# One decoder step on one core: first phi matrix loaded whole with its bias ahead of the loop, norm scaled in place, modulation in pairs of blocks, four activation sums moved into the compression

## The chip, the cores and the metric

The kernel runs on one core of a Trainium2 chip. The metric is device microseconds from the start to the end of one execution. The time of the kernel before is the median of three runs, 1209.62 us (1209.15 to 1214.17). One further execution was profiled, and all rows of views below are from it. Lines (L658) are lines of the kernel before, unless the text says of the kernel after. The engines: TensorE (PE; its weight loads PEld), VectorE (DVE), ScalarE (ACT), GpSimd (POOL) and SyncE (SP), which issues most DMAs.

## What is computed

One inference step of a decoder layer, in f32: 512 prompt tokens and 8 x 4 sample tokens, 1024 features, 16 heads over 4 KV heads. Only the first part of it bears on the change:

```python
sh1, sc1, g1, sh2, sc2, g2 = split(silu(c) @ w_ada + b_ada)
h  = rmsnorm(x, norm1) * (1 + sc1) + sh1
bg, cg, xin, q, kc, vc, ks, vs, kw, vw, nsa_g, merge_g = split_columns(h @ w_in)

def compress(rows, pe, w1, w2):          # k and v of 8 cached sequences of 1024 rows
    halves = rows in strides of 16       # block i = halves i and i + 1
    blocks = concat(halves[:-1], halves[1:]) + pe
    return gelu(flat(blocks) @ w1) @ w2
```

What follows (a gated short convolution, three attention branches, the output projections and a SwiGLU FFN) is the same in both kernels.

## The kernel before, in words

All activations lie feature-major: xT is [128, 8, 544], feature block k by token, and the 544 columns are worked in two halves, 288 and 256 wide (HS). Most f32 products are made of three products of a high and a low part: to_hilo copies the high part on ScalarE (L394) and subtracts it on VectorE (L395). Large products go by pairs of blocks in a scheme of seven half-block products (seven, L284), which needs four sums of quarters of the activation, S0 to S3 (T_ in the code), each 128x1088 with a high and a low part.

**The start.** SyncE issues the DMAs in an order written by hand (queue, L223). phi_load (L577) brings wphi[v], the first compression matrix for k (v = 0) or v (v = 1), 1.05 MB each; hp is a small slab with the position encodings, the second compression matrices and the conditioning input; cmp_gather (L617) brings the eight cached pages of a sequence (0.26 MB each) by the page table, those of sequence 0 half by SyncE and half by ScalarE's queue. wake(n) (L689) multiplies the identity by a 128x512 view of it n times, work with no result that runs before the first data are there.

**The compression** is a loop over 16 steps n = (sequence b, v). A step is 24 products of 128x128 on TensorE (cmp_M, L652): 16 of the pages by the two halves of wphi[v], and 8 of xs (the sum of odd and even strides, cmp_sum, L646, VectorE) by wsum[v] (the sum of the two halves of wphi[v], phi_sum, L582, VectorE). Then cmp_finish (L660) adds the bias on ScalarE, forms the blocks on VectorE and takes the gelu on ScalarE, and cmp_out2 (L677) multiplies by the second matrix. The bias is pe @ w1: phi_bias (L585) makes it with 16 products pb and a copy pbs on VectorE (L591), and phi_bias2 (L593) with one more product pbt and a copy into pbias (L597). Between the steps TensorE also makes the adaLN products (mod_slab), slab after slab as they arrive.

**Norm and modulation** run beside the steps 6 to 15: square_acc on blocks of xT, the inverse root (inv_from_sums, L440), its broadcast over partitions (inv_bcast, L474), and then modulate (L488), block by block and half by half: VectorE multiplies by the inverse root and A (md_u, L493), ScalarE adds the shift (Identity with a bias, L498), to_hilo writes h_h and h_l.

**Behind the compression** comes the linear product of the attention gates (L869, 48 products with gate's high and low weights, a sigmoid on ScalarE), and then the first kv pair by the seven-product scheme, whose weights (wslab, prepare) are brought and split into wh, wl, Wh, Wl. sum_1 stands in step 14, sum_2 in step 15 and sum_3 and sum_4 behind the loop. ScalarE loads a table whenever it changes between gelu and sigmoid.

What sets the order on an engine: a scheduler places the instructions of each engine in one row, by when it expects their inputs; the engine then takes the row in order. An instruction that waits holds up all that stand behind it on its engine.

Of the kernel before, what the change touches and what calls it, by code (L numbers as in the profile page):

```python
# [20 lines left out]
KC = 8  # L21
TP = 512
TS = 32
# [133 lines left out]
def build(tc, a, o):  # L157
# [419 lines left out]
    def phi_load(v, taps=slice(0, 2)):  # L577

        ks = slice(8 * taps.start, 8 * taps.stop)
        queue(lambda: sync.dma_start(wphi[v][:, ks], a["wt"][SLAB_AT[("phi", v)]].rearrange("p (k f) -> p k f", k=16)[:, ks]))  # L580
# [19 lines left out]
    gat = mkpool(gst, "gat", side="right")  # L600
    wsum = [gat.tile([128, 8, 128], F32, name=f"wsum{j}") for j in range(2)]
# [106 lines left out]
    T_, st = [], []  # L708

    def sum_1():  # L710
        st.append(raw_tile("raw")[:, 0:4 * WH].rearrange("p (k n) -> p k n", k=4))
        dve.tensor_sub(st[0], fq(0, 0), fq(0, 1))
        to_hilo(st[0], *T_[0])

    def sum_2():
        dve.scalar_tensor_tensor(st[0], st[0], -1.0, fq(1, 1), ALU.mult, ALU.subtract)
        to_hilo(st[0], *T_[1])

    def sum_3():
        st[0] = raw_tile("raw")[:, 0:4 * WH].rearrange("p (k n) -> p k n", k=4)  # L720
        dve.tensor_sub(st[0], fq(1, 1), fq(0, 1))
        to_hilo(st[0], *T_[2])

    def sum_4():
        dve.tensor_add(st[0], st[0], fq(0, 0))
        dve.tensor_sub(st[0], st[0], fq(1, 0))
        to_hilo(st[0], *T_[3])

    STEPS = [(b, v) for b in range(8) for v in range(2)]
    for n, (b, v) in enumerate(STEPS):  # L730
# [1299 lines left out]
```

## Time and profile before

| | |
|---|---|
| runs, median of three | 1209.62 us |
| runs, lowest and highest | 1209.15, 1214.17 us |
| profiled execution | 1209.88 us |
| its span in the trace | 1208.1 us |
| mean granted clock of TensorE | 0.998 |
| matmul records | 10114 |

The span runs from the first to the last thing in the trace. An f32 product shows as two matmul records. In a row of the timeline the first number is the start, the second the time from there to the end of the last of the records that it groups (xN), and the bracket at the end names how long the engine had been idle and what released it. In a row of groups the number behind the bar is the busy time in us, then the mean of one in ns, then the idle time ahead. In a row of windows each engine has its busy time and number of instructions, then come the granted clock, the DMA engines' share and GB/s.

### The profile page before, as it was taken

The numbers are of one execution on the slowest core, as the hardware profiler recorded it, in microseconds if no ns is written. First come the engines' busy times: TensorE is split into PE (matmuls) and PEld (weight loads), VectorE is DVE, ScalarE is ACT, GpSimd is POOL, SyncE is SP. The second block draws the span as 40 slices with busy tenths as digits, with TensorE's granted clock in tenths as the row PEclk, the third lists the DMA queues.
The fourth block names the chain that finished last, engine by engine and source line by source line (L and its number), as shares of the span: only waits on it lengthen the run. The fifth ranks groups of instructions, "written<-read, shape, count | busy, mean of one in ns | idle before, by whom it ended". The sixth has DMA issues, their size and how long they took to land. (4 is left out here: it accounts for less than half of the span.)

```text
span 1208.1 us, 25725 instructions
## 1 busy us (share of the span) xinstructions
PE 1191.2 (99%) x10114; PEld 1096.6 (91%) x10114; DVE 849.8 (70%) x1927; ACT 647.6 (54%) x1302; POOL 101.7 (8%) x154
## 2 busy tenths in 40 slices
PE   9999999999999999999999999999999999999997
PEld 7999999999999888787777879999999999999996
DVE  2539976888775576686767866758746877876776
ACT  1416544565456333386766765528555666666542
POOL 1000240000000111120101100000020001001000
PEclk9999999999999999999999999999999999999999
DMA  9953655889655998979887878534475359439512
GB/s 325 370 223 124 203 167 161 261 237 251 201 176 191 365 327 299 312 203 264 234 222 216 220 209 285 201 126 167 110 182 197 136 181 262 149 129 252 197 53 75
DMA packets 82251, 255.63 MB, mean 212 GB/s; under 512 B 9032, under 2 KB 17096, under 8 KB 67930
## 3 DMA queue, kind: packets, MB, share of 16 engines
q1 hardware_dynamic: 69442, 229.85, 54.5%
q0 software_dynamic: 12112, 23.09, 11.7%
q8 instruction: 79, 1.29, 0.4%
q10 hardware_dynamic: 576, 1.05, 0.3%
q14 instruction: 42, 0.34, 0.1%
HBM read 223.15 MB, written 65.28 MB: 239 GB/s over the span
## 5 line engine op out<-in xcount | busy, mean ns | idle before, releaser
L301 ACT ACTIVATE work<-wA 128x272 f32<-128x272 f32 x153 | 60.0, 392 | 85.3 <-PE wA L254 81.5
L395 DVE TENSOR_TENSOR Wl<-ws,Wh 128x1024 fp32r<-128x1024 f32 (+1 forms) x51 | 60.7, 1190 | 47.3 <-ACT Wh L394 44.0
L1417 ACT ACTIVATE P<-P,nms 128x384 f32<-128x384 f32 (+3 forms) x120 | 65.0, 543 | 19.8 <-DVE nms L1416 19.1
L1416 DVE CUSTOM_DVE_ANT_0 P<-sp,ta 128x384 f32<-128x384 f32 (+3 forms) x120 | 52.1, 468 | 30.0 <-PE sp L1404 22.8
L252 PE MATMUL lin<-h_h,wh 128*128 128x288 f32 (+1 forms) x240 | 71.5, 298 | 0.0
L395 DVE TENSOR_TENSOR wl<-ws,wh 128x1024 fp32r<-128x1024 f32 (+1 forms) x51 | 60.3, 1182 | 15.8 <-ACT wh L394 14.6
L253 PE MATMUL lin<-h_l,wh 128*128 128x288 f32 (+1 forms) x240 | 69.2, 289 | 0.0
L254 PE MATMUL lin<-h_h,wl 128*128 128x288 f32 (+1 forms) x240 | 68.9, 288 | 0.0
L394 ACT ACTIVATE wh<-raw 128x1024 fp32r<-128x1024 f32 (+2 forms) x55 | 55.4, 1007 | 24.1 <-PE wC L253 16.9
L394 ACT ACTIVATE Wh<-ws 128x1024 fp32r<-128x1024 f32 (+1 forms) x51 | 52.3, 1025 | 29.9 <-PE wC L253 29.2
L394 ACT ACTIVATE wh<-ws 128x1024 fp32r<-128x1024 f32 (+1 forms) x51 | 52.4, 1027 | 29.1 <-PE wB L253 27.4
L247 ACT ACTIVATE wh<-raw 128x1024 fp32r<-128x1024 f32 (+1 forms) x43 | 41.9, 973 | 43.3 <-PE lin L253 24.4
L395 DVE TENSOR_TENSOR wl<-raw,wh 128x1024 fp32r<-128x1024 f32 (+2 forms) x55 | 63.4, 1153 | 1.8 <-ACT wh L394 1.7
L658 PE MATMUL phi<-gt,wphi 128*128 128x128 f32 x512 | 61.4, 277 | 0.5 <-DMA gt<-in_cache_cmp 0.5
L658 PEld LDWEIGHTS phi<-gt,wphi 128*128 128x128 f32 x512 | 59.1, 192 | 2.7 <-DMA gt<-in_cache_cmp 1.3
L248 DVE TENSOR_TENSOR wl<-raw,wh 128x1024 fp32r<-128x1024 f32 (+1 forms) x43 | 48.2, 1121 | 16.9 <-ACT wh L247 16.4
L252 PE MATMUL wA<-S_hi,Wh 128*128 128x272 f32 x184 | 55.3, 301 | 1.7 <-ACT work L301 1.6
L557 POOL DMA_DIRECT2D pre<-in_wt x28 | 27.3, 977 | 331.0 <-DMA pre<-in_wt 331.0
L254 PE MATMUL wA<-S_hi,Wl 128*128 128x272 f32 x184 | 53.2, 289 | 0.0
L253 PE MATMUL wA<-S_lo,Wh 128*128 128x272 f32 x184 | 53.0, 288 | 0.0
L252 PEld LDWEIGHTS lin<-h_h,wh 128*128 128x128 f32 x240 | 45.6, 190 | 7.5 <-issue 6.2
L253 PEld LDWEIGHTS lin<-h_l,wh 128*128 128x128 f32 x240 | 45.2, 188 | 0.1
(583 smaller groups left out, 4365.6 us busy)
## 6 DMA issues: line engine op xcount, KB each, us to landing
raw<-in_wt SPq DMA_DIRECT2D x88, 1024.0 KB, 6.6
sraw<-in_cache_sel SPq DMA_DIRECT2D x64, 256.0 KB, 4.8
gt<-in_cache_cmp SPq DMA_DIRECT2D x60, 256.0 KB, 5.8
pre<-in_wt SPq DMA_DIRECT2D x20, 512.0 KB, 7.3
pre<-in_wt POOLq DMA_DIRECT2D x20, 512.0 KB, 7.1
ws<-pre SPq DMA_DIRECT2D x20, 512.0 KB, 3.4
raw<-in_wt SPq DMA_DIRECT2D x12, 768.0 KB, 5.7
wraw<-in_cache_winT SPq DMA_DIRECT2D x8, 1024.0 KB, 7.2
```

What stands on the lines that cost most here:

```text
L247: act.activation(oh, view, AF.Copy)
L248: dve.tensor_sub(ol, view, oh.bitcast(F32))
L252: pe.matmul(p, lhsT=wh[:, k, :], rhs=xh, start=start, stop=False, **kw)
L253: pe.matmul(p, lhsT=wh[:, k, :], rhs=xl, start=False, stop=False, **kw)
L254: pe.matmul(p, lhsT=wl[:, k, :], rhs=xh, start=False, stop=stop, **kw)
L301: o_.snap_ops.append(act.activation(t, p, AF.Copy))
L394: act.activation(hi, src, AF.Copy)
L395: return dve.tensor_sub(lo, src, hi.bitcast(F32))
L557: pool.dma_start(dst, src, accum_op=ALU.add)
L658: pe.matmul(po[:, c0:c0 + 128], lhsT=w[:, ch], rhs=x[:, :, ch * 16:ch * 16 + 16], start=(n_ == 0 and ch == 0), stop=(n_ == 2 and ch == 7))
L1416: p_ops.append(dve.tensor_tensor_reduce(out=t[:, 0:n], in0=sps[br], in1=t_dist[:, 512 - n:512], scale=-hs, scalar=3e38, op0=ALU.add, op1=A ...
L1417: e_ops.append(act.activation(t[:, 0:n], t[:, 0:n], AF.Exp, scale=-1.0, bias=nms[:, c:c + 1], accum_out=sums[:, c:c + 1]))
```

## The change

What it does, in the order of the program:

- phi_load brings wphi[0] whole and first; hp follows it, and then come the pages of sequence 0. Before, the first half of wphi[0] came ahead of the pages, and the second half and hp behind them.
- The bias of v = 0 is made ahead of the loop: five wakes, phi_sum(0), pb(0), two wakes, pbt(0), two wakes. Before, six and four wakes stood there, and both biases were made in steps 0 to 2.
- cmp_finish runs one step earlier (the list late is gone). Two of the gathered sequences (3 and 6) get a buffer in a pool of their own, gat2, which is closed at step 13.
- The squares are summed in steps 6 and 7, and the inverse root is taken at step 8. At step 9, xT is multiplied in place by the broadcast inverse root, two blocks at a time, for all tokens.
- modulate_x takes the place of modulate: ScalarE applies A and the shift in one Identity with a scale and a bias, and to_hilo runs once for two blocks.
- All four sums are made in the loop: S0 and S1 with their splits at step 13, S2 and S3 at step 14, the split of S3 at step 15. Each sum has a raw buffer ("st") of the three.

```diff
-    def phi_load(v, taps=slice(0, 2)):
-        ks = slice(8 * taps.start, 8 * taps.stop)
-        queue(lambda: sync.dma_start(wphi[v][:, ks], a["wt"][SLAB_AT[("phi", v)]].rearrange("p (k f) -> p k f", k=16)[:, ks]))
+    def phi_load(v):
+        queue(lambda: sync.dma_start(wphi[v].rearrange("p k f -> p (k f)"), a["wt"][SLAB_AT[("phi", v)]]))
...
-            t = gat.tile([128, 8, 512], F32, tag="gt", bufs=2, name=nm("gt"))
+            t = (gat2 if b in (3, 6) else gat).tile([128, 8, 512], F32, tag="gt", bufs=1, name=nm("gt"))
...
-    phi_load(0, slice(0, 1))
+    phi_load(0)
+    queue(lambda: sync.dma_start(hp, a["hp"]))
     cmp_gather(0)
-    phi_load(0, slice(1, 2))
-    queue(lambda: sync.dma_start(hp, a["hp"]))
     phi_load(1)
...
-    wake(6)
+    wake(5)
     phi_sum(0)
+    pb_ = phi_bias(0)
+    wake(2)
+    pb_()
     accs1 = [xp.tile([128, HW[hf]], F32, name=f"xacc{hf}") for hf in range(2)]
-    fins, late = [], []
+    fins = []
     xs_ = cmp_sum(0, 0)
-    wake(4)
+    wake(2)
...
+    def sums(i):
+        pool_ = mkpool(t7st, f"t7{i}")
+        T_.extend(sums_of(pool_, i + j) for j in range(2))
+        for j in range(2):
+            st[i + j] = raw_tile("st")[:, 0:4 * WH].rearrange("p (k n) -> p k n", k=4)
+        if i == 0:
+            dve.tensor_sub(raw_sum(0), fq(0, 0), fq(0, 1))
+            dve.scalar_tensor_tensor(raw_sum(1), raw_sum(0), -1.0, fq(1, 1), ALU.mult, ALU.subtract)
+        else:
+            dve.tensor_sub(raw_sum(2), fq(1, 1), fq(0, 1))
+            dve.tensor_add(raw_sum(3), raw_sum(2), fq(0, 0))
+            dve.tensor_sub(raw_sum(3), raw_sum(3), fq(1, 0))
+
+    def modulate_x(k, hf):
...
+        for kk in (k, k + 1):
+            act.activation(xT[:, kk, c], xT[:, kk, c], AF.Identity, scale=A1[:, kk, 0:1], bias=sh1[:, kk, 0:1])
+        ks = slice(k, k + 2)
+        to_hilo(xT[:, ks, c], hh_[:, ks, c], hl_[:, ks, c])
...
-        late.append((b, v, po))
-        if n < 2:
-            pb_ = phi_bias(n)
-            if n:
-                pb0()
-            pb0 = pb_
-        if n == 2:
-            pb0()
-        if n:
-            ready_ = late[:1] if n == 1 else late
-            late = late[len(ready_):]
-            fins = [cmp_finish(*z) for z in ready_]
+        if n == 0:
+            pb_ = phi_bias(1)
+        if n == 1:
+            pb_()
+        fins = [cmp_finish(b, v, po)]
...
+        if n == 8:
+            invs = [inv_from_sums(tok_sums(accs1[hf], hf), hf, xp) for hf in range(2)]
         if n == 9:
-            invs = [inv_from_sums(tok_sums(accs1[hf], hf), hf, xp) for hf in range(2)]
+            for hf in range(2):
+                inv = inv_bcast(invs[hf], hf, xp)
+                for k in range(0, KC, 2):
+                    xv = xT[:, k:k + 2, hcols(hf)]
+                    dve.tensor_mul(xv, xv, inv.rearrange("p (x n) -> p x n", x=1).broadcast_to([128, 2, HW[hf]]))
...
+        if n == 13:
+            gbst.close()
+            sums(0)
+            for i in range(2):
+                sum_split(i)
         if n == 14:
-            t7a = mkpool(t7st, "t7a")
-            T_ += [sums_of(t7a, 1), sums_of(t7a, 2)]
-            sum_1()
             wg = split(slab("gate"))
+            sums(2)
+            sum_split(2)
         if n == 15:
-            sum_2()
-            xst.close()
+            sum_split(3)
...
-    sum_3()
-    sum_4()
     linear(wg, h, lambda hf, p: act.activation(gT[0:48, hcols(hf)], p[0:48, :], AF.Sigmoid))
```

The change reorders three engines. The numbers behind the names below tell tiles of one name apart. On TensorE, at the start of the program, before (gt_1 is the pages of sequence 0, wphi0 the first phi matrix):

```order
L694 MATMUL wake_8_289<-ident_66 128x512 x6
L694 MATMUL wake_10_301<-ident_66 128x512 x4
L658 MATMUL phi_11_307<-gt_1_171,wphi0_156 128x128 x16
L658 MATMUL phi_11_307<-xs_9_299,wsum0_164 128x128 x8
L589 MATMUL pb_13_335<-wphi0_156,hp_158 32x128 x16
L658 MATMUL phi_15_354<-gt_1_171,wphi1_157 128x128 x16
```

And on TensorE at the same place in the kernel after:

```order
L693 MATMUL wake_8_291<-ident_66 128x512 x5
L587 MATMUL pb_9_298<-wphi0_156,hp_158 32x128 x16
L693 MATMUL wake_11_317<-ident_66 128x512 x2
L594 MATMUL pbt_12_320<-sel_159,pbs_10_315 128x1
L693 MATMUL wake_14_327<-ident_66 128x512 x2
L657 MATMUL phi_15_331<-gt_1_175,wphi0_156 128x128 x16
```

The products pb and pbt of the first bias moved from behind the first phi products to ahead of them; pbt reads pbs, the copy that VectorE makes. On VectorE, from its first instructions on, before (wphi1 is the second phi matrix):

```order
L696 TENSOR_REDUCE sel_159<-ident_66 128x1
L649 TENSOR_TENSOR xs_9_299<-gt_1_171 128x1024
L649 TENSOR_TENSOR xs_12_333<-gt_1_171 128x1024
L583 TENSOR_TENSOR wsum0_164<-wphi0_156 128x1024
L583 TENSOR_TENSOR wsum1_165<-wphi1_157 128x1024
L649 TENSOR_TENSOR xs_16_379<-gt_2_201 128x1024
L591 COPY pbs_14_352<-pb_13_335 128x128
```

And on VectorE in the kernel after:

```order
L581 TENSOR_TENSOR wsum0_167<-wphi0_156 128x1024
L695 TENSOR_REDUCE sel_159<-ident_66 128x1
L648 TENSOR_TENSOR xs_13_325<-gt_1_175 128x1024
L648 TENSOR_TENSOR xs_16_357<-gt_1_175 128x1024
L581 TENSOR_TENSOR wsum1_168<-wphi1_157 128x1024
L589 COPY pbs_10_315<-pb_9_298 128x128
L595 COPY pbias_160<-pbt_12_320 128x1
L648 TENSOR_TENSOR xs_23_416<-gt_2_203 128x1024
```

The copy pbs of the first bias stands directly behind the sum of the second phi matrix in the kernel after, and no longer behind the first sum of sequence 1. On ScalarE, around the end of the compression, before (raw_180 holds the first kv weights, lin the gate's two halves, Wh those of a weight sum):

```order
L394 ACTIVATE wh_181_1524<-raw_180_1522 128x1024
L674 ACTIVATE h1_177_1489<-t1_176_1483 128x128 x2
L394 ACTIVATE S3_hi_1507<-raw_185_1536 128x1088
L869 ACT_TABLE_LOAD
L869 ACTIVATE gT_96<-lin_186_1544 48x288
L394 ACTIVATE Wh_183_1530<-ws_178_1520 128x1024
L869 ACTIVATE gT_96<-lin_187_1570 48x256
```

And on ScalarE in the kernel after (raw_168 holds the first kv weights):

```order
L394 ACTIVATE S3_hi_1426<-st_161_1429 128x1088
L881 ACT_TABLE_LOAD
L881 ACTIVATE gT_96<-lin_173_1508 48x288
L673 ACT_TABLE_LOAD
L673 ACTIVATE h1_165_1470<-t1_164_1464 128x128 x2
L394 ACTIVATE wh_169_1496<-raw_168_1494 128x1024
L881 ACT_TABLE_LOAD
L881 ACTIVATE gT_96<-lin_174_1534 48x256
L394 ACTIVATE Wh_171_1502<-ws_166_1492 128x1024
```

The high part of the first kv weights, wh, moved from ahead of the last gelus to behind the first sigmoid, and two more table loads stand between.

More of the change, by code (lines that the diff above doesn't have):

```diff
@@ L600, in build @@
     gat = mkpool(gst, "gat", side="right")
+    gbst = ExitStack()
+    gat2 = mkpool(gbst, "gat2", side="right")
     wsum = [gat.tile([128, 8, 128], F32, name=f"wsum{j}") for j in range(2)]
@@ L707, in build, with sum_split @@
     fq = lambda k, q: xT[:, kq[k], Q[q]]
[L708 to L727, printed above, removed]
+    T_ = []
+    st = {}
+    raw_sum = lambda i: st[i]
+    def sums(i):
[10 more added lines that the diff above has]
+            dve.tensor_sub(raw_sum(3), raw_sum(3), fq(1, 0))
+    def sum_split(i):
+        to_hilo(raw_sum(i), *T_[i])
+    def modulate_x(k, hf):
+        c = slice(TS if hf == 0 else 288, 288 if hf == 0 else NT)
+        if k == 0 and hf == 0:
+            t4 = xT[:, :, 0:TS].rearrange("p k (b t) -> p k b t", t=4)
+            for z, op in ((A1, ALU.mult), (sh1, ALU.add)):
+                dve.tensor_tensor(t4, t4, z[:, :, 1:9].rearrange("p k (b x) -> p k b x", x=1).broadcast_to([128, KC, 8, 4]), op=op)
+            to_hilo(xT[:, :, 0:TS], hh_[:, :, 0:TS], hl_[:, :, 0:TS])
+        for kk in (k, k + 1):
+            act.activation(xT[:, kk, c], xT[:, kk, c], AF.Identity, scale=A1[:, kk, 0:1], bias=sh1[:, kk, 0:1])
+        ks = slice(k, k + 2)
+        to_hilo(xT[:, ks, c], hh_[:, ks, c], hl_[:, ks, c])
     STEPS = [(b, v) for b in range(8) for v in range(2)]
@@ L759, in build @@
             ordered[0] = False
-        if 6 <= n < 9:
-            for k in range(3 * n - 18, min(3 * n - 15, KC)):
+        if 6 <= n < 8:
+            for k in range(4 * n - 24, 4 * n - 20):
                 for hf in range(2):
                     square_acc(xT, k, hf, accs1[hf], xp, k == 0)
+        if n == 8:
+            invs = [inv_from_sums(tok_sums(accs1[hf], hf), hf, xp) for hf in range(2)]
         if n == 9:
-            invs = [inv_from_sums(tok_sums(accs1[hf], hf), hf, xp) for hf in range(2)]
+            for hf in range(2):
[3 more added lines that the diff above has]
+                    dve.tensor_mul(xv, xv, inv.rearrange("p (x n) -> p x n", x=1).broadcast_to([128, 2, HW[hf]]))
         if n == 10:
@@ L768, in build @@
             make_A(n1T, sc1, A1)
-            invs = [inv_bcast(invs[hf], hf, xp) for hf in range(2)]
             h = hh_, hl_ = tuple(hpool.tile([128, KC, NT], F32R, tag="h" + n_, bufs=1, name="h_" + n_) for n_ in "hl")
-            units = [u for hf in range(2) for u in [modulate(xT, invs[hf], A1, sh1, hh_, hl_, hf, xp, xT)] * KC]
-        for _ in range(4):
+            units = [(k, hf) for hf in range(2) for k in range(0, KC, 2)]
+        for _ in range(3):
             if units:
-                next(units.pop(0))
+                modulate_x(*units.pop(0))
+        if n == 12:
+            xst.close()
+        if n == 13:
[3 more added lines that the diff above has]
+                sum_split(i)
         if n == 14:
-            t7a = mkpool(t7st, "t7a")
-            T_ += [sums_of(t7a, 1), sums_of(t7a, 2)]
-            sum_1()
             wg = split(slab("gate"))
+            sums(2)
+            sum_split(2)
         if n == 15:
-            sum_2()
-            xst.close()
+            sum_split(3)
     gst.close()
@@ L859, in build @@
         pool.memset(t[:, 1024:1026], 0.0)
-    t7b = mkpool(t7st, "t7b")
-    T_ += [sums_of(t7b, 3), sums_of(t7b, 4)]
     q7st = ExitStack()
```

## The prediction

> **What bounds the kernel now.** I read the page first, then the windows of 100 us, then PE's waits in the first two of them, and only then the timeline of the places that the change touches.
>
> ```profile
> span 1208.1 us, 25725 instructions
> PE 1191.2 (99%) x10114; PEld 1096.6 (91%) x10114; DVE 849.8 (70%) x1927; ACT 647.6 (54%) x1302; POOL 101.7 (8%) x154
> ```
>
> TensorE is busy in 1191.2 of 1208.1 us, 16.9 us less than the span. A change gains where it closes one of these gaps or takes matmuls away, and loses wherever it makes TensorE stand. The windows (PE, PEld, DVE, ACT, POOL, then PE's clock, DMA share and GB/s) and PE's waits (total, times, longest) say where it stands in the stretch that is changed:
>
> ```profile
> 0.00:100.00 100.00, 98.01 (x1019) 86.22 (x1020) 43.97 (x132) 27.42 (x79) 5.06 (x14) 1.00 0.77 285
> 100.00:200.00 100.00, 97.54 (x820) 94.80 (x819) 83.19 (x131) 53.84 (x98) 21.51 (x26) 1.00 0.56 169
> 120.00:140.00 20.00, 18.92 (x153) 17.93 (x152) 19.76 (x29) 12.06 (x20) 1.36 (x3) 1.00 0.57 165
> PE wake L694 <- POOL ident masks.py:199: 1.5, 1, 1.5
> PE phi L658 <- DMA gt<-in_cache_cmp: 0.5, 1, 0.5
> PE wA L252 <- ACT work L301: 2.1, 3, 1.0
> PE wA L254 <- DVE wl L395: 0.4, 1, 0.4
> ```
>
> In the first 100 us TensorE stands for 2.0 us, 1.5 of them before its first instruction. In the second 100 it stands for 2.46 us: three waits of wA on ScalarE's work (2.1) and one on VectorE (0.4). So what the change gives VectorE and ScalarE can win about 2.5 us, no more, unless TensorE is held up inside its busy time. VectorE is full in 120 to 140 (19.76 of 20), which is where the relief is aimed. What the start can lose has no such bound. The timeline of the start:
>
> ```profile
> 1.47 10.93 PE L694 MATMUL wake<-ident 128*128 128x512 f32 x20 [1.47 <-POOL ident masks.py:199]
> 4.20 0.33 PEld L694 LDWEIGHTS wake<-ident 128*128 128x128 f32 x1 [0.52 <-issue]
> 5.05 0.33 PEld L694 LDWEIGHTS wake<-ident 128*128 128x128 f32 x1 [0.52 <-issue]
> 6.23 0.19 PEld L694 LDWEIGHTS wake<-ident 128*128 128x128 f32 x1 [0.24 <-issue]
> 6.66 0.19 PEld L694 LDWEIGHTS wake<-ident 128*128 128x128 f32 x1 [0.24 <-issue]
> 10.23 0.33 SPq L580 DMA_DIRECT2D wphi<-in_wt  x1
> 12.90 2.36 DVE L649 TENSOR_TENSOR xs<-gt 128x1024 f32<-128x1024 f32 x2 [11.29 <-DMA hp<-in_hp]
> 12.92 3.84 PE L658 MATMUL phi<-gt,wphi 128*128 128x128 f32 x32 [0.52 <-DMA gt<-in_cache_cmp]
> 17.67 1.23 DVE L583 TENSOR_TENSOR wsum<-wphi 128x1024 f32<-128x1024 f32 x1 [1.28 <-DMA wphi<-in_wt]
> 18.48 1.08 PE L589 MATMUL pb<-wphi,hp 128*32 128x128 f32 x32
> 19.49 3.84 PE L658 MATMUL phi<-gt,wphi 128*128 128x128 f32 x32
> 24.63 0.28 DVE L591 COPY pbs<-pb 128x128 f32<-128x128 f32 x1
> 26.05 0.38 PE L596 MATMUL pbt<-sel,pbs 128*128 128x1 f32 x2
> 26.30 3.82 PE L658 MATMUL phi<-gt,wphi 128*128 128x128 f32 x32
> ```
>
> Ten wake matmuls (two records each) run up to the first product of the compression. That starts at 12.92, when the pages are there. Since TensorE's only two waits up to 100 us are those above, whatever delays 12.92 moves the whole program.
>
> **The start.** The first phi matrix is loaded whole ahead of the pages, and its bias is made ahead of the loop. Two places of the order decide. On TensorE, pbt(0) now stands ahead of the first phi product, with two wakes ahead of it and two behind. On VectorE, the copy pbs(0) that pbt(0) reads stands *behind* wsum1, the sum of the halves of the second phi matrix. So the first product now waits for the landing of the second matrix, which it does not read.
>
> When does that land? In before its sum starts at 17.67 (that row is released by its DMA). It was issued at 10.23 behind one whole wphi0, hp and eight pages. In after the same bytes stand ahead of it in another order, so I keep 17.67, with an estimate of 15 to 18.7 for what the new order may do: at the early end because whole loads need fewer turns of SP, at the late end because SP now gets to the pages later. Then wsum1 takes 1.23 and pbs 0.28: pbt(0) can start at 17.67 + 1.51 = 19.2.
>
> What TensorE does until then: the twenty records of ten wakes end at 12.4 (1.47 + 10.93); five wakes are ten records of 0.43 (6.23 to 6.66) fewer, and end at about 8.1. Then pb(0) takes 1.01 (18.48 to 19.49), and two wakes four records of 0.43, 1.7 us. That is over at about 10.8, later if hp is later; the stand is some 6 to 8.5 us. Does the clock hold over it? At the end of the kernel it does not:
>
> ```profile
> 1200.26 0.42 PE L1910 MATMUL yt<-ident,x1b 128*128 128x128 f32 x2
> 1200.70:1203.70 3.00, 0.00 (x0) 0.00 (x0) 2.63 (x11) 1.50 (x3) 0.70 (x1) 1.00 0.56 197
> 1203.80:1208.10 4.30, 0.00 (x0) 0.00 (x0) 0.00 (x0) 0.00 (x0) 0.00 (x0) 0.50 0.63 241
> ```
>
> The last matmul ends at 1200.68. The granted clock is 1.00 up to 1203.70 and 0.50 from 1203.80, 3.1 us after it. A stand of 6 to 8.5 us is twice that, so I take it that the clock has halved by 19.2. At the start, where it is half, a record takes 0.85 us (4.20 to 5.05), and the quicker spacing of 0.43 begins between 5.05 and 6.23, some 4.2 us after the first wake.
>
> [...]
>
> So: pbt(0) at 19.2 takes 0.4 at half clock, and two wakes 4 x 0.85 = 3.4, which makes 23.0. The clock opens some 4.2 us after 19.2, at 23.4, and the first 0.4 us of the product at half speed lose 0.2: 23.2 in effect, against 12.92, is 10.3 us. Off that goes what no longer stands in the loop: pb(0), 1.01, and pbt(0), 0.25 (26.05 to 26.30). The start costs 10.3 - 1.26 = **+9.0 us**. TensorE has no wait between there and 100 us that could take any of it back.
>
> The bounds. With the clock held open, two wakes cost 1.7: 19.2 + 0.25 + 1.7 = 21.2, so 8.2 - 1.26 = +7.0. With an early landing, VectorE must still sum the pages first: 12.90 + 2.36 = 15.26, then 1.23 + 0.28 = 16.8, and with the clock open 18.7: 5.8 - 1.26 = +4.5. Landing at 18.7 gives +10.0. A gain is excluded, since two wakes and the pbt stand behind a copy that cannot end before 16.8.
>
> The sums of the pages, wsum0 and the gathers of later sequences lie beside this stand and cost nothing. They have no slack to lose either, as everything that reads them is moved by the same 9 us.
>
> **The modulation.** The rows by form on VectorE between 88 and 140 us, a 128x576 row from the end of the kernel (each of four near 753 ns), and the ScalarE rows:
>
> ```profile
> L493 DVE SCALAR_TENSOR_TENSOR md_u<-xT,A,inv 128x256 f32<-128x256 f32 x16 | 7.4, 476 | 0.1
> L395 DVE TENSOR_TENSOR h_l<-xT,h_h 128x256 fp32r<-128x256 f32 x17 | 6.5, 416 | 0.3 <-ACT h_h L394 0.3
> L331 DVE TENSOR_TENSOR ws<-raw 128x512 f32<-128x512 f32 x1 | 0.7, 680 | 0.0
> L395 DVE TENSOR_TENSOR S_lo<-raw,S_hi 128x1088 fp32r<-128x1088 f32 x4 | 5.1, 1282 | 0.0
> L1920 DVE TENSOR_TENSOR x1b<-x1b,ys x4: 751/753/772, 1195.2 to 1201.0; 128x576 f32<-128x576 f32 x4
> L498 ACT ACTIVATE xT<-md_u,modT 128x256 f32<-128x256 f32 x16 | 7.7, 501 | 2.0 <-DVE md_u L493 1.7
> L674 ACT ACTIVATE h<-t 128x128 f32<-128x128 f32 x12 | 3.4, 314 | 0.8 <-DVE t L667 0.7
> ```
>
> VectorE loses 16 x 0.476 = 7.6 and 16 x 0.416 = 6.7, 14.3 us. It gets four in-place products 128x2x288 at 0.753 and four 128x2x256 at 0.680, 5.7, and eight differences 128x512 at 0.680, 5.4: 11.1 us. The balance is -3.2 us. ScalarE keeps 16 Identity; no row shows one with both a scale and a bias read per partition, and I bound it by 0.50 (the row with a bias) and 0.6. ScalarE is busy 12.06 of 20 us there, so that stays hidden. On TensorE's path this part is worth nothing by itself.
>
> **The four sums within the compression.** They are nine passes of 128x1088 on VectorE (five sums and four S_lo), 1.28 each. In before five of them end after TensorE has left the compression at 122.6, 6.4 us; now all nine are queued ahead of the first kv weights. VectorE was nearly full there before, so I expect it not to be 6.4 us ahead afterwards, but 1 to 3. Which waits does that close? And what does ScalarE do meanwhile?
>
> ```profile
> 122.60 0.40 PE L252 MATMUL lin<-h_h,wh 128*128 128x288 f32 x1
> 122.89 1.05 ACT L394 ACTIVATE wh<-raw 128x1024 fp32r<-128x1024 f32 x1
> 126.19 1.28 ACT L869 ACT_TABLE_LOAD   x1
> 127.49 0.40 ACT L869 ACTIVATE gT<-lin 48x288 f32<-48x288 f32 x1
> 129.01 0.28 PE L254 MATMUL wA<-h_h,wl 128*128 128x272 f32 x1
> 135.72 0.39 PE L252 MATMUL wA<-S_hi,Wh 128*128 128x272 f32 x1 [0.59 <-ACT work L301]
> 137.98 0.39 PE L252 MATMUL wA<-S_hi,wh 128*128 128x272 f32 x1 [0.49 <-ACT work L301]
> ```
>
> The waits at 135.72 and 137.98 are of work that stood behind S_hi and wl of the late sums; 1.08 us go. Of the other two, 1.0 and 0.4 later on, I count half, 0.7.
>
> But ScalarE's order has a new knot. The first kv weight's wh, which ran at 122.89, is now queued behind S3_hi, a table load, the sigmoid of gate half 0, a second table load and the two gelus of the last step. In before's times: the gate's 48 products run evenly from 122.60 to just ahead of wA's first three, the third of which is the row at 129.01. Half 0 is 24 of them, a little longer than the others, and ends at about 126.1. So gT to 126.6, the load 1.28 to 127.9, two gelus of 0.31 to 128.5, wh 1.05 to 129.5, and wl on VectorE, one pass of 128x1024 (two took 2.36 at 12.90), to 130.8. That is what wA's third product waits for. That is a new wait of about 1.8 us, less (1.2) if the gate's half is seen sooner, more (3) if S3_hi itself is late and the first load shows too.
>
> [...]
>
> Together this stage is -1.08 - 0.7 + 1.8 = **0.0 us**, from -1.3 to +2.
>
> The compression's finish and the inverse root each run one step earlier. Both move VectorE work into steps where it is under half busy (43.97 of 100 us), and cost nothing. What changes in the pools takes no wait away from TensorE, as it shows none there.
>
> **The sum.** The profiled execution took 1209.88 us (span 1208.1 and 1.8 around it), the median of the runs is 1209.62, 0.26 less. 1209.88 + 9.0 + 0.0 - 0.26 = **1218.6 us**.
>
> **The rivals.** A, the clock stays open over the stand: +7.0, so 1216.6. For it, the stand may be as short as 6 us; against, 3.1 us were enough at the end. 0.10.
>
> B, the second phi matrix lands before VectorE has summed the pages, below 15.3 us: +4.5, so 1214.1. For it, SP has fewer turns to take and the last pages of sequence 0 no longer stand between two pieces of wphi0; against, 4.3 MB (two matrices of 1.05, eight pages of 0.26, hp) took until 17.67 before. 0.09.
>
> C, the other side: TensorE's busy time between 100 and 140 hides stalls that full VectorE causes, and the whole relief, 3.2 + 6.4 = 9.6 us, comes through on TensorE: 1218.6 - 9.6 = 1209.0, or 1204.5 with the least start. It decides only if it is worth more than the start, from about 6 us on. Against it, 2.46 us are all the gaps there are, and the products there follow each other at an even spacing. 0.04.
>
> [...]
>
> The forecast keeps 0.70.
>
> **How the numbers follow.** A measurement of this kernel can tell about 0.5% from no change, 6 us: 1203.6 and 1215.7. The forecast ends above 1215.7 except for 0.03 of its 0.70 (a landing between B's and 17), A for 0.08 of 0.10, D always: slower 0.67 + 0.08 + 0.07 = 0.82. Same: 0.03 + 0.02 + 0.09 (B) + 0.02 of C = 0.16. Faster: 0.02, the rest of C. The range reaches from B, 1214.0, to the latest landing with the stage at its worst, 1218.6 + 1.0 + 2 = 1221.6, put at 1221.5; C and a part of D are left out.
>
> **What would show it.** In the profile after: a wait of TensorE at pbt before its first phi product of 6 us or more, released by VectorE's copy; wsum1 directly ahead of that copy, released by the DMA of wphi; the wakes behind it at 0.85 us a record; the first phi product near 23 instead of 12.92; a new wait of wA near 138 us on wh or wl of ScalarE and VectorE; the waits on work at 135.72 and 137.98 gone. I am wrong if pbt runs before 16 us, if TensorE's gaps in 100 to 200 us shrink by more than 2.5 us, or if the busy time of the compression itself changes.

## The result and the profile after

The kernel after takes 1223.53 us (median of six runs, 1220.03 to 1225.79). The kernel before takes 1211.57 us in six runs, the three shown ahead and three more. The ratio is 1.0096, with a 95% interval from 1.0076 to 1.0117: 11.6 us slower (12.0 by the two medians). The direction and the cause named first were right. The time lies 2 us above the range, which ended at 1221.5. The profiled execution is the quickest of the six, 1220.03 us. Of all the runs in this document one, of e8, took 2320.06 us; it stands far apart from the rest and is left out of the times and ratios.

The head of the page of the kernel after:

```profile
span 1218.3 us, 25700 instructions
PE 1194.9 (98%) x10112; PEld 1099.2 (90%) x10112; DVE 846.7 (69%) x1910; ACT 649.8 (53%) x1296; POOL 102.2 (8%) x154
```

Its windows of 100 us:

```profile
0.00:100.00 100.00, 93.05 (x957) 80.32 (x958) 39.68 (x114) 22.56 (x65) 5.08 (x14) 0.97 0.73 278
100.00:200.00 100.00, 97.34 (x794) 94.52 (x793) 78.72 (x123) 57.17 (x99) 21.00 (x25) 0.98 0.52 164
```

And TensorE's waits in them:

```profile
PE pbt L594 <- DVE pbs L589: 5.5, 1, 5.5
PE wA L252 <- ACT work L301: 1.5, 1, 1.5
PE wA L252 <- ACT wh L394: 1.2, 1, 1.2
```

VectorE is busy 4.3 us less in the first 100 us and 4.5 us less in the second. Most of that is work that comes later, as everything is moved back: over the whole span it is 3.1 us less (846.7 instead of 849.8). TensorE stands longer all the same: 7.0 us in the first hundred instead of 2.0, 2.7 in the second instead of 2.5. The clock is below 1.00 in both. The start of the kernel after:

```profile
1.48 7.17 PE L693 MATMUL wake<-ident 128*128 128x512 f32 x10 [1.48 <-POOL ident masks.py:199]
9.59 1.98 PE L693 MATMUL wake<-ident 128*128 128x512 f32 x4
13.25 2.36 DVE L648 TENSOR_TENSOR xs<-gt 128x1024 f32<-128x1024 f32 x2 [5.93 <-DMA gt<-in_cache_cmp]
15.57 1.23 DVE L581 TENSOR_TENSOR wsum<-wphi 128x1024 f32<-128x1024 f32 x1
16.71 0.28 DVE L589 COPY pbs<-pb 128x128 f32<-128x128 f32 x1
17.05 0.59 PE L594 MATMUL pbt<-sel,pbs 128*128 128x1 f32 x2 [5.47 <-DVE pbs L589]
17.50 3.41 PE L693 MATMUL wake<-ident 128*128 128x512 f32 x4
20.74 3.73 PE L657 MATMUL phi<-gt,wphi 128*128 128x128 f32 x32
```

TensorE stands for 5.47 us at pbt, which waits for the copy pbs. Ahead of the copy on VectorE are the two page sums and wsum1, with no gap between. So here the second phi matrix had landed by 15.57, not at 17.67. The two wakes behind pbt take 3.41 us, about 0.85 us a record, the half-clock price (the granted clock is 0.50 from 13.59 to 20.42). The first product starts at 20.74 instead of 12.92.

The end of the compression and what follows, on ScalarE:

```profile
131.31 1.12 ACT L394 ACTIVATE S_hi<-st 128x1088 fp32r<-128x1088 f32 x1 [0.39 <-DVE st L725]
132.44 1.28 ACT L881 ACT_TABLE_LOAD   x1
133.74 0.40 ACT L881 ACTIVATE gT<-lin 48x288 f32<-48x288 f32 x1
134.16 1.28 ACT L673 ACT_TABLE_LOAD   x1
135.45 0.52 ACT L673 ACTIVATE h<-t 128x128 f32<-128x128 f32 x2
135.87 1.04 ACT L394 ACTIVATE wh<-raw 128x1024 fp32r<-128x1024 f32 x1
```

The same stretch on TensorE:

```profile
129.48 0.40 PE L252 MATMUL lin<-h_h,wh 128*128 128x288 f32 x1
136.96 0.39 PE L252 MATMUL wA<-h_h,wh 128*128 128x272 f32 x1 [1.18 <-ACT wh L394]
138.52 0.39 PE L254 MATMUL wA<-h_h,wl 128*128 128x272 f32 x1
158.84 0.39 PE L252 MATMUL wA<-S_hi,Wh 128*128 128x272 f32 x1 [1.48 <-ACT work L301]
```

And three windows of 3.41 us behind that last stand (PE's clock is the third figure from the end):

```profile
156.95:160.36 3.41, 1.93 (x14) 1.49 (x13) 3.41 (x5) 0.40 (x1) 1.96 (x2) 1.00 0.94 206
160.37:163.77 3.40, 3.40 (x18) 3.40 (x17) 1.13 (x2) 0.68 (x2) 2.19 (x3) 0.50 0.01 2
163.78:167.18 3.40, 3.40 (x29) 3.40 (x29) 3.04 (x4) 2.09 (x4) 1.33 (x2) 1.00 0.18 66
```

The knot on ScalarE is there in the forecast order: S3_hi, load, sigmoid, load, gelus, wh. Behind a stand of 1.48 us comes something that the prediction did not have. The clock halves for one window, 160.37 to 163.77, in which 18 records run instead of 29.

Same places in both kernels, as a table (us; the lag is after less before):

| place | before | after | lag |
|---|---|---|---|
| first phi product | 12.92 | 20.74 | 7.8, of which 1.3 is given back as pb and pbt leave the loop |
| gate's first product | 122.60 | 129.48 | 6.9 |
| third product of wA (first to read wl) | 129.01 | 138.52 | 9.5 |
| first product of kvt (behind the products of the kv weights) | 225.32 | 233.90 | 8.6 |
| end of the span | 1208.1 | 1218.3 | 10.2 |

### The profile page after: what moved, and what is told of

Read it like the earlier page. It is cut to its first block, busy times and chain, and to the rows that moved or that the text cites. A ratio compares the mean times of both kernels' runs of the same rounds, so it can differ in the third digit from the quotient of the medians.

```text
span 1218.3 us, 25700 instructions
## 1 busy us (share of the span) xinstructions
PE 1194.9 (98%) x10112; PEld 1099.2 (90%) x10112; DVE 846.7 (69%) x1910; ACT 649.8 (53%) x1296; POOL 102.2 (8%) x154
## 4 chain that ended last, share of the span: by engine, by line
PE 52%; DVE 3%; DMA 2%; ACT 1%; issue 0%; POOL 0%; SPq 0%; DVEq 0%; ACTq 0%; POOLq 0%
PE lin L253 4%; PE lin L254 4%; PE lin L252 4%; PE wA L252 4%; PE wA L254 4%; PE wA L253 4%; PE acc L1450 3%; PE ptp L1456 3%; PE wC L254 2%; PE wC L253 2%; PE wC L252 2%; PE modp L414 1%; PE dn L254 1%; PE dn L252 1%; PE dn L253 1%; DMA gb<-gb_dr 1%
## 5 line engine op out<-in xcount | busy, mean ns | idle before, releaser
L648 DVE TENSOR_TENSOR xs<-gt 128x1024 f32<-128x1024 f32 x16 | 19.5, 1223 | 40.6 <-PE phi L657 32.6
```

## The experiments

Twelve runs follow (no run is labelled e6). Ratios are to the kernel before, timed on the same chip side by side (medians from 1211.5 to 1212.3 us); 0.1% is 1.2 us. A ratio is not the quotient of the two medians; the two differ by up to 0.0009, 1 us. The lag is read in each profile against that of the kernel before, at the gate's first product (122.60 before) where nothing else is said. That one profile of the kernel before is a quick execution (1209.88), so lags at the end of the span come out some 1 to 3 us too large.

**e1, only wsum1 behind the copy.** In the kernel after:

```diff
-            phi_sum(1)
+            with tc.issue_after(pbs_op[0].ins):
+                phi_sum(1)
```

> The kernel after, with only the sum wsum1 put behind the copy pbs(0) in VectorE's row; the sums xs of the pages stay ahead of the copy. Theory S (the copy's place in VectorE's row sets the start): pbt can start at about 15.8 instead of 17.05, since only the one pass wsum1 of 1.23 us leaves; the clock is still half; the first phi product near 19.5 instead of 20.74; 1.2 us faster than the kernel after. Rival L (the new load order sets the start: whole matrix ahead of the pages): pbt moves, but the first product stays near 20.7 or the gain is nil.

```profile
14.96 0.28 DVE L591 COPY pbs<-pb 128x128 f32<-128x128 f32 x1
15.30 0.59 PE L596 MATMUL pbt<-sel,pbs 128*128 128x1 f32 x2 [4.89 <-DVE pbs L591]
19.30 4.79 PE L659 MATMUL phi<-gt,wphi 128*128 128x128 f32 x32
```

1218.96 us, ratio 1.0054 (1.0036 to 1.0072). pbt moved by 1.75 us and the product by 1.44, as theory S has it, a little more than forecast because the page sums started earlier (12.69 instead of 13.25). The product itself then took 4.79 us, since the clock was still half when it began (its mean is 0.73 from 10 to 20 us and 0.92 from 20 to 30). In time e1 is 0.26% below e9, more than these 1.4 us, though the intervals overlap.

**e2, the copy ahead of all sums.** e1 with the page sums of steps 0 and later put behind the copy:

```diff
-    xs_ = cmp_sum(0, 0)
+    with tc.issue_after(pbs_op[0].ins):
+        xs_ = cmp_sum(0, 0)
...
-            xs_ = cmp_sum(*STEPS[n + 1])
+            with tc.issue_after(pbs_op[0].ins):
+                xs_ = cmp_sum(*STEPS[n + 1])
```

> The kernel after, with the copy pbs(0) ahead of all sums of pages and of wsum1 in VectorE's row; loads, wakes and the middle as in the kernel after. Theory S: pbt runs at about 10 us, two wakes end at about 12, and the first phi product starts when the pages are there, 13.3, with the clock open: 7.4 us earlier than in the kernel after, so 7.4 us faster than it and 2 to 4 us slower than the kernel before (what the middle costs). Rival L: the loads hold the first product to 15 us or more, and it gains 5 us at most. If the clock still halves in the gap of 1.3 us, the product starts at 13.3 at half speed, and 1.5 us are lost.

```profile
9.89 0.29 DVE L591 COPY pbs<-pb 128x128 f32<-128x128 f32 x1 [2.39 <-PE pb L589]
13.52 3.73 PE L659 MATMUL phi<-gt,wphi 128*128 128x128 f32 x32
24.31 1.23 DVE L650 TENSOR_TENSOR xs<-gt 128x1024 f32<-128x1024 f32 x1 [4.97 <-DMA gt<-in_cache_cmp]
28.07 0.69 PE L683 MATMUL ph<-h,hp 128*64 128x126 f32 x4 [2.47 <-ACT h L675]
```

The clock behind that stand, in windows, and the window of a later stand of 1.47 us:

```profile
24.17:27.57 3.40, 1.43 (x13) 1.24 (x12) 3.23 (x7) 1.35 (x2) 0.00 (x0) 1.00 0.92 324
27.59:30.99 3.40, 2.92 (x15) 2.60 (x16) 1.02 (x5) 1.45 (x6) 0.00 (x0) 0.50 0.98 358
31.00:34.40 3.40, 3.40 (x18) 3.40 (x17) 0.00 (x0) 0.26 (x2) 0.00 (x0) 0.50 0.99 395
153.88:157.29 3.41, 1.94 (x15) 1.72 (x15) 3.41 (x4) 1.11 (x2) 1.87 (x3) 1.00 1.04 250
157.30:160.70 3.40, 3.40 (x26) 3.18 (x26) 2.52 (x5) 0.66 (x2) 3.27 (x4) 1.00 0.30 98
```

1213.62 us, ratio 1.0011 (1.0000 to 1.0022). The stand at pbt is gone and the first product runs at 13.52 with the clock open (1.00 from 10 to 20 us), so theory S holds and rival L falls: the loads were not what held the start. A new stand came in its place. VectorE now waits with the page sums of sequence 1 in hand, which land at 24.3, and the finish of step 0 is queued behind them. The finish had been moved one step earlier, so TensorE reaches its gelu's product early and stands 2.47 us. Two windows at half clock follow, and the lag in this execution is 5.2 us at the gate. The profiled run is one of the two slowest of twelve (1216.57; all lie between 1211.1 and 1217.0). Seven of the twelve have a mean clock of 0.997 or 0.998, like the kernel before, which leaves no room for two windows at half clock; in those the stand is not there, is shorter, or leaves the clock alone. The forecast "2 to 4 us slower than the kernel before" was too high: it is 1.3 (0.0 to 2.7), with the knot on ScalarE still in it (the profile shows its table loads at 130.72 and 132.44).

**e3, the old start with the new middle.** The kernel after with phi_load in halves, ten wakes, both biases in the loop and the finish one step later, all as in the kernel before.

```diff
-    wake(5)
+    wake(6)
     phi_sum(0)
-    pb_ = phi_bias(0)
-    wake(2)
-    pb_()
...
-    wake(2)
+    wake(4)
```

> The kernel after with the whole start of the kernel before (halves of the first matrix, ten wakes, both biases in the loop, the finish one step later); modulation and sums as in the kernel after. Theory M (the middle costs by itself: table loads ahead of the first kv weight 2.6, less 2.5 of waits removed, and a stand of 1.5 us near 157 that halves the clock once, 1.5 us more): first phi product at 12.9, and 1 to 3.5 us slower than the kernel before, with the clock dip again. Rival P (the middle is neutral, and what the kernel after loses behind 150 us comes from the shift of 6.7 us against the loads): within 0.5 us of the kernel before, without a dip.

1210.95 us, ratio 0.9996 (0.9982 to 1.0010). The middle alone costs nothing that can be told, and no dip of the clock shows in the profile, with 1.00 in every 10 us up to 1200 (one of the twelve runs, 1218.04 us, has a mean clock of 0.993). But it has no knot either: with the earlier start the scheduler put the last gelus ahead of the sigmoid, and one table load is left (at 126.09, gT at 127.38, wh at 127.69). So e3 tells what the middle is worth without the two extra loads, and that is nothing. Theory M is open as far as the knot goes.

**e4, the new start with the old middle.** The kernel before with the start's part of the diff and nothing else.

```diff
-    wake(6)
+    wake(5)
     phi_sum(0)
+    pb_ = phi_bias(0)
+    wake(2)
+    pb_()
...
-        late.append((b, v, po))
+        fins = [cmp_finish(b, v, po)]
```

> The kernel before with the new start alone (whole matrix first, first bias ahead of the loop, finish one step earlier); modulation and sums as in the kernel before. Theory S with M: the first phi product at 20.7, 6.7 us slower than the kernel before, and the waits behind 120 us as in the kernel before (0.6, 0.5, 1.0, 0.4). Rival P: 9 us or more slower, with a new stand near 157 and a dip of the clock.

1218.06 us, ratio 1.0048 (1.0032 to 1.0064): 5.8 us. The first product runs at 20.84 and the lag is 6.7 us from 49 to beyond 500 us, with the four waits of the kernel before. The stand near 157 is the kernel before's wait of 1.0 us, and no dip follows it (the clock is 1.00 from 150 to 180 us). The profiled execution shows 9.9 at its end, 3 us of it in waits behind 600 us, but the timed runs don't bear these out.

**e5, the knot untied.** The kernel after with the sigmoids behind the last gelu and behind wh:

```diff
+    def gate(hf, p):
+        with tc.issue_after(his[n_hi].ins), tc.issue_after(gelu[0].ins):
+            act.activation(gT[0:48, hcols(hf)], p[0:48, :], AF.Sigmoid)
...
-    linear(wg, h, lambda hf, p: act.activation(gT[0:48, hcols(hf)], p[0:48, :], AF.Sigmoid))
+    linear(wg, h, gate)
```

> The kernel after with ScalarE's row mended at one place: the gate's sigmoids stand behind the last gelus and behind wh of the first kv weight, so that one table load is left there instead of three. Theory M (the two extra loads hold wh): the wait of wA on wh (1.18 us) and the wait on wl behind it, 2.6 us together, go, and 2 to 2.6 us come off the kernel after, with the dip near 160 as it was or moved. Rival G (the gain is given back at the next weights, which VectorE cannot split sooner): the wait goes, but waits of wA on work or wl between 140 and 165 grow, and less than 1 us comes off. The raw weights land at 132.7, so wh can't start earlier than that.

```profile
135.90 1.05 ACT L396 ACTIVATE wh<-raw 128x1024 fp32r<-128x1024 f32 x1
136.97 1.28 ACT L889 ACT_TABLE_LOAD   x1
138.26 0.67 ACT L889 ACTIVATE gT<-lin 48x288 f32<-48x288 f32 x2
```

TensorE's waits from 100 to 300 us in e5:

```profile
PE wA L254 <- DVE wl L397: 0.7, 1, 0.7
```

1218.72 us, ratio 1.0053 (1.0038 to 1.0068). The kernel after, timed side by side with it (e9), has 1.0080, so untying is worth 0.27%, 3.3 us, by the ratios, but the two intervals overlap, and by the medians it is 1.6 us. In the profile these waits fall to the one of 0.7. Nothing was given back at the next weights (rival G).

**e7, both repairs of the start and the untied knot.** e2 and e5 together, and the page sums of sequence 1 behind the finish of step 0:

```diff
-            with tc.issue_after(pbs_op[0].ins):
+            with tc.issue_after((fin_op if n else pbs_op)[0].ins):
                 xs_ = cmp_sum(*STEPS[n + 1])
```

> The kernel of e2 (copy first) with two more repairs: the sums xs of sequence 1 stand behind the finish of step 0 on VectorE (in e2 the finish stood behind them, TensorE waited 2.5 us for its gelu at 25.6, and its clock was half from 27.6 to 34.8), and ScalarE's row as in e5. Theory: the lag against the kernel before is -0.7 us at 100 us (first phi product at 13.5, less 1.26 of bias products), and 1 to 3 us faster than the kernel before in all. Rival: the repairs only move the stand to the pages of sequence 1 (landing at 24.3), the lag stays above +1, and the time is that of the kernel before or slower.

```profile
13.19 3.81 PE L661 MATMUL phi<-gt,wphi 128*128 128x128 f32 x32 [0.42 <-issue]
25.28 0.44 PE L687 MATMUL ph<-h,hp 128*64 128x126 f32 x4
```

A wait on ScalarE's work is the longest from 100 to 300 us:

```profile
PE wA L252 <- ACT work L301: 2.0, 1, 2.0
```

The windows around it:

```profile
148.62:152.02 3.40, 1.75 (x13) 1.71 (x14) 3.40 (x6) 0.40 (x1) 3.31 (x3) 1.00 0.83 192
152.03:155.43 3.40, 3.40 (x29) 3.40 (x29) 2.07 (x3) 2.14 (x4) 2.06 (x3) 1.00 0.04 9
```

1210.21 us, ratio 0.9991 (0.9980 to 1.0001): 1.1 us quicker than the kernel before, not quite clear of none. The lag is -0.6 us at the gate. So what the change costs is in these three places, pbt's wait, the finish and the knot: with all three mended, nothing of the 11.6 us is left. From e2, which has the mended pbt alone and was timed at another time, to e7 it is 0.20%, 2.4 us, for the finish and the knot together. The middle has less to do for VectorE, and TensorE still stands, now once for 2.0 us instead of three times for 2.1 in all.

**e8, wakes that last.** The kernel after with eight wakes ahead of pbt; the scheduler untied the knot here too.

```diff
     pb_ = phi_bias(0)
-    wake(2)
+    wake(8)
     pb_()
```

> The kernel after with eight wakes instead of two ahead of pbt, which keep TensorE busy to about 16.8 us, as long as VectorE's copy takes. (The scheduler also puts wh ahead of the gate's table load here, as in e5.) Theory C (a part of the start's price is the clock that halves in the stand): pbt at 17.05 as before, the two wakes behind it at 0.43 a record instead of 0.85, the first phi product at 19.0 instead of 20.74, and a lag of 5.2 instead of 6.9 at 100 us. Rival: the clock is no part of it, and the first product stays at 20.7.

```profile
17.47 0.38 PE L594 MATMUL pbt<-sel,pbs 128*128 128x1 f32 x2 [1.48 <-DVE pbs L589]
17.72 1.96 PE L693 MATMUL wake<-ident 128*128 128x512 f32 x4
19.52 3.73 PE L657 MATMUL phi<-gt,wphi 128*128 128x128 f32 x32
```

1216.70 us (median of five runs), ratio 1.0044 (1.0030 to 1.0058). pbt came 0.4 us later than in the kernel after, the two wakes behind it took 1.8 instead of 3.2, and the product started 1.2 us earlier. Theory C holds: from pbt to the product 2.05 us against 3.69, so 1.6 us of the start's price is the clock, whose mean from 10 to 20 us is 1.00 here and 0.68 in the kernel after.

**e9, the kernel after again**, unchanged, timed side by side with e5, e7 and e8.

> The kernel after, unchanged, timed beside the three others of this call. Its six runs lay between 1220.0 and 1225.8 us, while e1, which starts 0.5 us earlier, came out at 1219.0. If the two kernels differ by more than their starts, 1223 us again (1.0096 of before); if it was a matter of the runs, 1219 to 1220 (1.006).

```profile
16.42 1.23 DVE L581 TENSOR_TENSOR wsum<-wphi 128x1024 f32<-128x1024 f32 x1 [1.31 <-DMA wphi<-in_wt]
17.90 0.59 PE L594 MATMUL pbt<-sel,pbs 128*128 128x1 f32 x2 [6.50 <-DVE pbs L589]
21.91 4.27 PE L657 MATMUL phi<-gt,wphi 128*128 128x128 f32 x30
```

1220.28 us (1219.11 to 1226.59), ratio 1.0080 (1.0060 to 1.0100), between the two cases. In this execution wsum1 is released by the landing of wphi, at 16.42, which is the wait that the prediction had. The clock halves later and is half until 23.5 us instead of 20.4, so that the first product's records begin at half speed, and the lag is 8.8 us. The same start in e5 (the second phi matrix at 16.85, the first product at 22.32) has 9.6. So one and the same start costs 6.7 (e4) to 9.6 us, by how the transfers land and when the clock opens. The longer runs of e9 have a lower mean clock: 0.995 in those of 1219 to 1221 us, 0.994 in the one of 1222.43, 0.992 in the one of 1226.59. One window of 3.41 us more at half clock makes 0.0014 of that and costs 1.7 us at most, an estimate from its length, so the clock explains less than the 7 us between them.

**e10, the repaired start with the old middle.** e4 with the repairs of e7 on VectorE.

```diff
+            with tc.issue_after(pbs_op[0].ins):
+                phi_sum(1)
...
+            with tc.issue_after((fin_op if n else pbs_op)[0].ins):
+                xs_ = cmp_sum(*STEPS[n + 1])
```

> The kernel before with the repaired start alone: whole first matrix, first bias ahead of the loop, finish one step earlier, copy pbs(0) ahead of the page sums, sums of sequence 1 behind the first finish; modulation and activation sums as in the kernel before. Theory: lag -0.4 to -0.7 us at 100 us and the same to the end, ratio 0.9995. Rival: what made e7 about 1 us faster than the kernel before is in the middle, and this one is the kernel before or slower.

1210.93 us, ratio 0.9994 (0.9985 to 1.0003), with a lag of -0.5 us. e7 differs from it by the middle alone, without the knot, and has 0.9991, so again the middle is worth nothing that can be told.

**e11, the modulation alone.** The kernel before with the in-place scaling and modulate_x, and the four sums where they were (sequences 3 and 6 have their own buffer, as in the kernel after).

```diff
-            units = [u for hf in range(2) for u in [modulate(xT, invs[hf], A1, sh1, hh_, hl_, hf, xp, xT)] * KC]
+            units = [(k, hf) for hf in range(2) for k in range(0, KC, 2)]
...
-                next(units.pop(0))
+                modulate_x(*units.pop(0))
```

> The kernel before with the new modulation alone (xT scaled in place, two blocks at a time, squares and inverse root earlier); start and the four sums as in the kernel before. Theory: VectorE has 3.2 us less to do by 120 us, TensorE's four waits on ScalarE's work and wl (0.6, 0.5, 1.0, 0.4) shrink to 1 us or less, ScalarE's row keeps its one table load, and it is 1 to 1.5 us faster than the kernel before. Rival: the waits between 135 and 165 stand on transfers and GpSimd's copies, not on VectorE's sum of work, and stay at 2.0 us or more: no difference.

1212.42 us, ratio 1.0010 (0.9997 to 1.0022): no gain. The scheduler made three table loads of it here, with wh ahead of them. TensorE's waits in 100 to 300 us came to 1.8 us, less than 2.5, but the end is 1.4 us later in the profile, by waits on wl behind 600 us. Such waits are longer in every other profile than in that of the kernel before.

**e12, the probe.** The kernel before with a stand behind each of twelve steps; the stands are extra work whose result nothing reads.

```diff
+            dve.tensor_copy(scr, po[:, 256:384])
+            for _ in range(2 * ((n - 2) % 6)):
+                dve.tensor_add(scr, scr, ident)
+            probe[0] = pe.matmul(tp_ps(nm("probe"))[:, 0:128], lhsT=scr, rhs=ident, start=True, stop=True)
```

> The kernel before with twelve stands put into the compression: behind the products of steps 2 to 13 a copy and 0, 2, 4, 6, 8 or 10 additions on VectorE, and a product of TensorE on their result, ahead of the next step's products. Stands of about 0.5 to 4 us. Theory W (the clock is decided by windows of 3.4 us that run free, and halves behind a window with more than some 1.4 us of stand): stands under 1.4 us never halve it, those over 2.8 us always do, those between do or don't by where they fall, and each half stretch is 3.4 us or a multiple of it. Rival F (only a window that is all idle halves it): no stand under 3.4 us does.

Two of the stands, in windows of 3.41 us that follow the clock's own changes:

```profile
38.21:41.62 3.41, 1.20 (x10) 0.98 (x9) 2.49 (x8) 0.47 (x1) 0.00 (x0) 1.00 1.04 439
41.63:45.03 3.40, 3.40 (x23) 3.02 (x22) 0.42 (x1) 0.67 (x3) 0.00 (x0) 0.50 1.02 440
45.04:48.44 3.40, 3.40 (x32) 3.40 (x32) 0.00 (x0) 0.00 (x0) 0.00 (x0) 1.00 0.14 56
89.41:92.82 3.41, 1.70 (x16) 1.50 (x14) 1.68 (x4) 0.47 (x1) 0.00 (x0) 1.00 0.02 2
92.83:96.23 3.40, 0.19 (x2) 0.23 (x2) 2.89 (x13) 0.64 (x2) 0.00 (x0) 1.00 0.00 0
96.24:99.64 3.40, 3.40 (x41) 2.38 (x41) 0.10 (x1) 0.55 (x2) 0.00 (x0) 0.50 0.00 0
```

1279.54 us, one run. The changes of the clock at 41.63, 45.04 and 96.24 lie 1 and 15 times 3.413 us apart. In the first stand TensorE is idle in 65% of a window, and the next window is at half clock. The window from 89.41 holds the first part of a longer stand; it is idle in 50%, and the clock stays at 1.00 until the end of the next one, which is idle in 94% and is followed by half clock. Rival F falls: neither of the two windows ahead of half clock was idle throughout. Theory W holds for the grid and for the longer stand. Its threshold of 1.4 us (41%) is too low for this run, where 50% passed, and what a stand of 1.5 us does was not tried: the twelve stands measure 0.38 us (two) or 2.21 and more.

**e13, a delay alone.** The kernel before with more wakes ahead of everything:

```diff
-    wake(4)
+    wake(12)
```

> The kernel before with eight wakes more at the start (18 instead of 10), which move TensorE's first product by 8 x 0.86 = 6.9 us with the clock open and nothing else at the start changed. Theory R (a delay at the start is handed through whole and no more, as nothing behind it waits longer): lag 6.4 to 6.9 us at 100 us and at the end, ratio 1.0055. Rival D (the waits behind 600 us, which were 1 to 3 us longer in e4 than in the kernel before, come from the delay itself): lag 8 to 10 at the end, ratio 1.007 to 1.008.

1219.41 us, ratio 1.0058 (1.0043 to 1.0072), 7.0 us for a delay of 6.8 (first product at 19.76). Theory R holds in the timed runs: a delay of the first product is handed through whole, and no more, though the interval just takes in 1.007, where rival D begins. (The profiled execution shows 8.6 at its end, with waits behind 600 us like those of e4.)

## Why the prediction failed, point by point

**What bounds the kernel**: right. Whatever delays the first product moves the program (e13: 6.8 us in, 7.0 out), and VectorE's relief meets at most the few waits there are.

**The place of the start's cost**: right, and shown by e2. pbt stands behind a copy that VectorE takes only behind the page sums and wsum1; with the copy first, the product runs at 13.52. The wait is 5.47 us in the profile and 6.50 in e9, where the prediction's sign was 6 or more.

**The landing of the second phi matrix**: mis-sized. "So I keep 17.67" came out at 15.57 or before in the first profile, at 16.42 in e9 and at 16.85 in e5. All lie within the estimate of 15 to 18.7, and rival B was nearer in the first.

**The clock**: right in kind. It halved (0.50 from 13.59 to 20.42), and the wakes took 0.85 us a record. It is worth 1.6 us by e8, where the prediction's two cases differ by 2.0.

**The start's term, +9.0**: 2.1 us too large in the profile of the kernel after, where the lag at the gate is 6.9, because the second phi matrix landed 2.1 earlier. But the four profiles with this start have 6.7, 6.9, 8.8 and 9.6, and 9.0 is among them by some luck: in e9 an earlier landing and a clock that opens late make up for each other. In time, the start alone costs 5.8 us (e4, 3.9 to 7.8), while e2, which takes it out of the kernel after, has 0.69% less than e9, 8.4 us. The term is right in kind and its size stays open within that. It was not too small, so it is not what put the time above the range.

**The stage's term, 0.0**: held, from -1.3 to +2. From the gate's first product to the first of kvt the profiles have (us, and more or less than the kernel before):

| run | ScalarE's row | gate to kvt | against before |
|---|---|---|---|
| before | | 102.72 | |
| after | knot | 104.42 | +1.7, with a window at half clock |
| e9 | knot | 102.14 | -0.6 |
| e1, e2 | knot | 103.28, 103.34 | +0.6, +0.6 |
| e3, e5 | untied | 101.56, 100.48 | -1.2, -2.2 |
| e7, e8 | untied | 102.34, 101.14 | -0.4, -1.6 |

The knot came as forecast and larger, with wl done at 138.2 and the third product 2.6 us late instead of 1.8, and what the stage gives back was larger too. By these rows the knot costs some 2 us, an estimate from the means of the two kinds; by the timed runs 1.6 to 3.3 (e5), and not more than 2.4 from e2 to e7. Without it the middle is worth nothing that the timed runs can tell (e3 0.9996; e7 against e10). The waits at 135.72 and 137.98 went, but the waits on work did not all go: one of 1.5 us stands in the profile of the kernel after, one of 2.0 in e7, and 0.2 in e9.

**The table loads**: each took 1.28, and what is behind it started within 0.02 us (132.44 and 133.74). Rival D, which the sums of the chances count at 0.07, is that ScalarE's order costs more than counted. No run shows the term that it would add; what the profile of the kernel after shows is the third product of wA 2.6 us late instead of 1.8.

**The finish one step earlier**, costed at nothing: right in the kernel after, whose late start covers it, and wrong without that cover. In e2 it is a stand of 2.47 us and two windows at half clock. The prediction named VectorE's free time as the cover; what counted was the finish's place in the row, behind a sum that waits for pages.

**The clock in the stage**: not in the prediction at all. It took the clock as something that only a long stand can close. A stand of 1.48 us near 157 brought a window at half clock, 18 records in place of 29, which costs 3.4 x (1 - 18/29) = 1.3 us. It is in the profile of the kernel after and not in that of e9. Nor is it in e2, where a stand of 1.47 us at the same place of the program leaves the clock open (153.88 to 160.70).

The recorded changes of the clock lie on a grid of 3.413 us: in the kernel after at 6.77, 13.59, 20.42, 160.37, 163.78 and 1211.67, which is 2, 2, 41, 1 and 307 times 3.413 us from one to the next, and in the kernel before at 5.69 and 1203.77, 351 times. The idle share of a window that was enough for half clock to follow differs: 91% in the kernel before (1200.36 to 1203.76), 65 and 94% in e12, 58% in e2, and in the kernel after 59% (10.18 to 13.59), 43% (156.95 to 160.36) and, in the program's last window with products, 47% (1208.26 to 1211.67). But 43% in e2, 49% in e7, 50% in e12 and 54% in e9 (9.84 to 13.25; its mean clock of 0.83 from 10 to 20 us puts the halving one window later) were not. So between 43 and 54% both happen, and the idle share alone does not decide; what else does is not shown.

**The sum: the step that failed** is its base. The sum starts from a median of 1209.62 us of three runs, and the range gives it no spread. The six runs timed with the kernel after have 1211.57, 1.95 us more, and the time passes the range by 2.03.

The change itself is 11.6 us (9.2 to 14.2) where 9.0 was forecast, 1.0096 instead of 1.0074. In the profile of the quickest run the 10.2 us at the end are 6.9 of the start, 1.7 of the stage, where the clock's window was put at nothing, and 1.6 behind kvt, also put at nothing. That last part is hardly the change's doing: behind kvt every profile but the probe's, not compared here, is 0.9 to 3.1 us slower than the one profile of the kernel before from which the prediction started, also in kernels whose timed runs are no slower (e10 1.3, e3 3.0).

What stays open is what the other five runs of the kernel after have more than the profiled one, 1 to 6 us, as none of them has a profile. The clock tells little of it: the mean clock is 0.993 in the quickest run and 0.992 in the slowest, and 0.995 in two between. Open too is why the kernel came out 3 us quicker when it was timed again (e9, 1220.28, which lies in the range).

## What to carry to other kernels

When a product is moved ahead, read the whole row of the engine that makes its operand: in e9 a copy of 0.28 us stood behind a sum that waited for a transfer until 16.42, and TensorE stood 6.50 us for the copy. A table function moved by a scheduler among others of another table can cost more than the work that was saved (here two more loads of 1.28 us each and some 2 us in all, against nothing that could be told), so look at the row of ScalarE and not only at the sums. And a forecast in microseconds needs the spread of the base in its range; three runs of this kernel put its median 0.16% below that of six, and the one profile was a quick execution too.

## What the runs showed of the hardware

The granted clock changed on a grid of 3.413 us in the profiles of both kernels and in e12. A stand of 1.5 to 2.5 us cost nothing more (2.0 us in e7, at 49% of a window) or some 3 us more (2.47 us in e2, two windows at half clock; an estimate from the lag of 5.2 there and of -0.6 in e7, less the stand itself). How much of a window it fills, and so where it falls on the grid, counts (the windows of 58% and more named above were each followed by half clock), but does not settle it: stands of 1.47 us in e2 and 1.48 in the kernel after fill 43% of a window each, and only the second was followed by half clock. In e2 a window with 0.48 us of stand in it (27.59 to 30.99) did not open the clock again, and one without any (31.00 to 34.40) did, with 1.00 from 34.41.
